# Bias addition and row maximum in one VectorE instruction, in the first block's attention

## The chip, the cores and the metric

The kernel runs on one core of one Trainium2 chip. The metric is device microseconds (us) of one execution. Engines are named as in the profile: PE is TensorE (PEld its weight load), DVE is VectorE, ACT is ScalarE, POOL is GpSimd and SP is SyncE, which issues most DMAs.

## The reference

A feed-forward layer, an attention layer, a second feed-forward layer and an embedding gate make up the first block; a second block of two layers follows. The change lies in the attention of the first block: 256 tokens, 16 heads of width 64. Heads 0 to 7 (mixer A) look at the last 128 tokens, share two key heads, and have a learned sink logit each; heads 8 to 15 (mixer B) merge three dilated windows.

```
logits = q @ k.T * 64 ** -0.5 + bias          # bias by distance, masked places at -1e30
m = max(logits)                               # mixer A: max(m, sink)
p = exp(logits - m)                           # mixer A: the denominator gets exp(sink - m) too
out = (p @ v) / sum(p)
att = concat(out of 16 heads) @ w_out + b_out
h = h + rms_norm(att, attn_post_g)
```

## The kernel before, in words

Everything is in f32. A projection is three matmuls per tile, on a high and a low part of each operand. `units` loads 128 x 2 x 512 of a weight by an SP DMA into one of four `raw` buffers, ACT rounds the high part (`whi`, L115) and DVE subtracts it (`wlo`, L116), into 16 `whl` buffers.

Attention of the first block (`attention1`) works in eight jobs of two heads: jobs 0 to 3 are mixer A (with the sink), jobs 4 to 7 mixer B. A job runs through these steps:

- `scores`: four matmuls into two PSUM tiles `S` (L443), one for each head, the first token tile in columns 0 to 127, the second in 128 to 383. DVE adds the bias and mask table `btab` (read backwards along the row) into `L` (L447, four instructions, two of 128 and two of 256 columns), takes row maxima (L449, one per token tile for both heads), takes the larger of that and the sink (L453, two instructions, mixer A alone), and negates (`nm`, L454). ACT takes exps with the row sums into `den` (L460, four). For mixer A the sink's exp joins `den` (L464 to L466). DVE takes the reciprocal `rc` (L468) and normalizes `L` (L473, four).
- `turn_p`, some time after: TensorE transposes `L` (L185) into a PSUM tile `trP`, three blocks a head, and ACT copies it to `pT` (L483).
- `apply`, after that: TensorE multiplies by the values into PSUM `O` (L491, L492); ACT and DVE split `O` into `mixh` (L190) and `mixl` (L191).

Behind jobs 0 to 3 two more projections each are put in (`fill`: q and k of mixer B, `z`). After the jobs come the matmuls with `w_out` (`wo`, L126 to L128): the first half of their inputs (jobs 0 to 3) for three of the four output tiles, then the second half, which needs jobs 4 to 7. Each output tile is finished by a bias addition on DVE (`att`, L571), and each token tile then goes through a norm into the next layer.

The PSUM tiles `S`, `O`, `z` and `wo` share six buffers (`mm`), `trP` has two (`tr`). When a step is issued, is set in the program by a clock that counts matmul rows (`spend`, `defer`, `WAIT`); the framework's scheduler then fixes one order of instructions for each engine when the program is built, by its own estimate of when each can start. The engines run these orders as they stand.

Of the kernel before, what the change touches and what calls it, by code (L numbers as in the profile page):

```python
# [14 lines left out]
ALU = mybir.AluOpType  # L15
AX = mybir.AxisListType.X
# [10 lines left out]
NEG = -1e30  # L27
# [15 lines left out]
class Net:  # L43
# [360 lines left out]
    def attention1(self, hs, norm, nxt):  # L404
        nc, a = self.nc, self.a
        X = norm.X
        snk = self.work.tile([P, 8], F32, name="snk", tag="snk", bufs=1)
# [24 lines left out]
        def scores(j, qT, kT, kj, sink):  # L432


            b0 = 2 * j if sink else 8 + 2 * j
            L = self.k4("L", [P, 2, 384])
            m = self.sm("m", 4)
            ps = [self.mm("S") for _ in range(2)]
            cs = [slice(0, 128), slice(128, 384)]
            for t in range(2):  # L440
                for i in range(2):
                    r = slice(64 * i, 64 * i + 64)
                    nc.tensor.matmul(ps[i][:, cs[t]], qT[r, j, t * P:(t + 1) * P], kT[r, kj, 0:128 * (t + 1)], start=True, stop=True)  # L443
            for t in range(2):
                for i in range(2):
                    b = b0 + i
                    nc.vector.tensor_tensor(out=L[:, i, cs[t]], in0=ps[i][:, cs[t]],  # L447
                                            in1=self.btab[b // 4][:, b % 4, 0:128 * (1 + t)][:, ::-1], op=ALU.add)
                nc.vector.tensor_reduce(out=m[:, 2 * t:2 * t + 2], in_=L[:, :, cs[t]], axis=AX, op=ALU.max)  # L449
            nm = self.sm("nm", 4)  # L450
            if sink:
                for t in range(2):
                    nc.vector.tensor_tensor(out=m[:, 2 * t:2 * t + 2], in0=m[:, 2 * t:2 * t + 2], in1=snk[:, 2 * j:2 * j + 2], op=ALU.max)  # L453
            nc.vector.tensor_scalar(out=nm, in0=m, scalar1=-1.0, scalar2=None, op0=ALU.mult)  # L454
            den = self.sm("den", 4)
            for t in range(2):
                o = slice(0, 128) if t == 0 else slice(128, 384)
                for i in range(2):
                    c = 2 * t + i
                    nc.scalar.activation(L[:, i, o], L[:, i, o], AF.Exp, bias=nm[:, c:c + 1], accum_out=den[:, c:c + 1])  # L460
            if sink:
                es = self.sm("es", 4)
                for t in range(2):
                    nc.vector.tensor_tensor(out=es[:, 2 * t:2 * t + 2], in0=nm[:, 2 * t:2 * t + 2], in1=snk[:, 2 * j:2 * j + 2], op=ALU.add)  # L464
                nc.scalar.activation(es, es, AF.Exp)
                nc.vector.tensor_tensor(out=den, in0=den, in1=es, op=ALU.add)  # L466
            rc = self.sm("rc", 4)
            nc.vector.reciprocal(rc, den)  # L468
            for t in range(2):
                o = slice(0, 128) if t == 0 else slice(128, 384)  # L470
                for i in range(2):
                    c = 2 * t + i
                    nc.vector.tensor_scalar(out=L[:, i, o], in0=L[:, i, o], scalar1=rc[:, c:c + 1], scalar2=None, op0=ALU.mult)  # L473
            return L
# [57 lines left out]
        def job(sa, ap):  # L532
            L = scores(*sa)
            self.spend(1900)

            def turn():
                pT = turn_p(L)
                self.clock += 0.7
                self.defer(lambda: apply(pT, *ap), WAIT["pv1"])

            self.defer(turn, WAIT["soft1"])
# [21 lines left out]
        for t in range(2):  # L563
            for n in range(2):
                ps = early.get((t, n))
                if ps is None:
                    ps = self.mm("wo")
# [957 lines left out]
```

## Time and profile before

| | us |
|---|---|
| three runs | 1761.73, 1761.76, 1766.66 (median 1761.76) |
| the profiled execution, its own time | 1764.69 |
| its span in the trace | 1761.7 |
| TensorE busy | 1721.5 |
| VectorE busy | 1248.3 |
| ScalarE busy | 864.4 |

The span is what the rows cover; the 3.0 us between it and the profiled execution's own time lie outside the trace. The attention stage of the first block lies between about 238 and 305 us of the span. A time in a row is counted from the span's start. A line number (L447) is that of the kernel's text; the kernel after has two lines fewer in `scores`, so that its L452 is L454 of before, L458 is L460, L471 is L473, L481 is L483 and L569 is L571.

### The profile page before, as it was taken

How to read it: one execution, taken by the hardware profiler on the slowest of the kernel's cores; microseconds unless marked ns; L12 is line 12 of the kernel's file. 1: busy time of each engine (PE TensorE's matmuls, PEld its weight loads, DVE VectorE, ACT ScalarE, POOL GpSimd, SP SyncE). 2: the span in 40 equal slices, each digit the busy share in tenths (PEclk: the TensorE clock that was granted, in tenths of full speed). 3: DMA queues.
4: the chain of work that ended last, by engine and by line, in shares of the span. 5: the costliest groups of instructions: out<-in, count | busy, mean ns of one | idle time of the engine just before them, and what ended most of it. 6: DMA issues, size and time to landing. Idle time of an engine off the chain costs nothing.

```text
span 1761.7 us, 26817 instructions
## 1 busy us (share of the span) xinstructions
PE 1721.5 (98%) x9910; PEld 1503.5 (85%) x9910; DVE 1248.3 (71%) x2467; ACT 864.4 (49%) x1809; POOL 49.4 (3%) x77
## 2 busy tenths in 40 slices
PE   7999999999999999999999999999999999999998
PEld 5998897889888888888878888887889988979997
DVE  6766778976769897687657886456659858775554
ACT  6444557654567442456425333333337446664443
POOL 0000000000001000110000000000000001000000
PEclk9999999999999999999999999999999999999999
DMA  7756644675564437422545566564334553465563
GB/s 271 256 196 205 216 153 144 217 251 197 171 205 149 145 134 261 152 85 84 191 168 179 190 224 232 174 217 155 116 124 143 167 191 124 147 225 195 186 202 111
DMA packets 96435, 315.14 MB, mean 179 GB/s; under 512 B 11006, under 2 KB 18608, under 8 KB 96304
## 3 DMA queue, kind: packets, MB, share of 16 engines
q1 hardware_dynamic: 94448, 309.73, 51.8%
q10 hardware_dynamic: 1856, 3.70, 0.6%
q8 instruction: 77, 1.26, 0.3%
q14 instruction: 54, 0.44, 0.1%
HBM read 300.76 MB, written 12.63 MB: 178 GB/s over the span
## 4 chain that ended last, share of the span: by engine, by line
PE 84%; DVE 6%; DMA 5%; ACT 2%; issue 2%; POOL 1%; SPq 0%; POOLq 0%; ACTq 0%; DVEq 0%
PE f2u L139 3%; PE f2u L141 3%; PE f2u L140 3%; PE f2dn L126 3%; PE f2g L139 3%; PE f2g L141 3%; PE f2g L140 3%; PE f2dn L128 3%; PE f2dn L127 3%; DVE wlo L116 2%; PE O L1145 2%; PE trP L185 1%; PE q L128 1%; PE q L126 1%; PE hy L139 1%
## 5 line engine op out<-in xcount | busy, mean ns | idle before, releaser
L116 DVE TENSOR_TENSOR wlo<-raw,whi 128x512 fp32r<-128x512 f32 x844 | 545.7, 683 | 149.0 <-ACT whi L115 106.4
L115 ACT ACTIVATE whi<-raw 128x512 fp32r<-128x512 f32 x844 | 492.8, 624 | 168.2 <-PE f2dn L128 29.6
L661 DVE SCALAR_TENSOR_TENSOR wmod<-wmod,crow 128x1024 f32<-128x1024 f32 x96 | 116.1, 1219 | 2.0 <-DMA wmod<-in_w_modT_dram 1.8
L126 PE MATMUL f2dn<-whi,f2ah 128*128 128x512 f32 x264 | 103.6, 392 | 0.0
L139 PE MATMUL f2g<-fxh,whi 128*128 128x512 f32 (+1 forms) x304 | 103.1, 339 | 0.0
L140 PE MATMUL f2g<-fxl,whi 128*128 128x512 f32 (+1 forms) x304 | 103.0, 339 | 0.0
L141 PE MATMUL f2g<-fxh,wlo 128*128 128x512 f32 (+1 forms) x304 | 103.0, 339 | 0.0
L139 PE MATMUL f2u<-fxh,whi 128*128 128x512 f32 (+1 forms) x304 | 103.0, 339 | 0.0
L140 PE MATMUL f2u<-fxl,whi 128*128 128x512 f32 (+1 forms) x304 | 103.0, 339 | 0.0
L141 PE MATMUL f2u<-fxh,wlo 128*128 128x512 f32 (+1 forms) x304 | 103.0, 339 | 0.0
L128 PE MATMUL f2dn<-whi,f2al 128*128 128x512 f32 x264 | 102.8, 389 | 0.0
L127 PE MATMUL f2dn<-wlo,f2ah 128*128 128x512 f32 x264 | 102.7, 389 | 0.0
L661 DVE SCALAR_TENSOR_TENSOR mjunk<-wmod,crow 128x1024 bf16<-128x1024 f32 x64 | 77.4, 1219 | 10.9 <-DMA wmod<-in_w_modT_dram 10.7
L141 PE MATMUL hy<-lxh,wlo 128*128 128x256 f32 (+1 forms) x224 | 69.7, 315 | 0.1
L140 PE MATMUL hy<-lxl,whi 128*128 128x256 f32 (+1 forms) x224 | 69.6, 314 | 0.0
L139 PE MATMUL hy<-lxh,whi 128*128 128x256 f32 (+1 forms) x224 | 69.2, 316 | 0.0
L190 ACT ACTIVATE f2ah<-f2s 128x512 fp32r<-128x512 f32 (+1 forms) x40 | 21.3, 532 | 91.3 <-DVE f2s L288 91.2
L285 ACT ACTIVATE f2s<-f2g 128x512 f32<-128x512 f32 (+1 forms) x38 | 18.9, 496 | 95.2 <-PE f2g L141 95.2
L288 DVE TENSOR_TENSOR f2s<-f2u,f2s 128x512 f32<-128x512 f32 (+1 forms) x38 | 21.4, 562 | 60.7 <-PE f2u L141 60.7
L140 PEld LDWEIGHTS f2g<-fxl,whi 128*128 128x128 f32 x304 | 57.7, 190 | 6.3
L141 PEld LDWEIGHTS f2u<-fxh,wlo 128*128 128x128 f32 x304 | 57.7, 190 | 6.3
L139 PEld LDWEIGHTS f2u<-fxh,whi 128*128 128x128 f32 x304 | 57.7, 190 | 6.2
(527 smaller groups left out, 4785.4 us busy)
## 6 DMA issues: line engine op xcount, KB each, us to landing
wmod<-in_w_modT_dram SPq DMA_DIRECT2D x96, 512.0 KB, 6.4
raw<-in_ffn_w_gu_dram SPq DMA_DIRECT2D x88, 512.0 KB, 4.6
raw<-in_w_gate_up_dram SPq DMA_DIRECT2D x88, 512.0 KB, 5.9
raw<-in_w_in_dram SPq DMA_DIRECT2D x80, 512.0 KB, 5.1
raw<-in_ffn_w_down_dram SPq DMA_DIRECT2D x44, 512.0 KB, 4.6
raw<-in_w_down_dram SPq DMA_DIRECT2D x44, 512.0 KB, 4.0
raw<-in_w_out_dram SPq DMA_DIRECT2D x24, 512.0 KB, 4.7
raw<-in_w_in_q_dram SPq DMA_DIRECT2D x16, 512.0 KB, 5.1
```

Source lines behind the costliest of these rows:

```text
L115: nc.scalar.activation(hi, raw[:, j], AF.Copy)
L116: nc.vector.tensor_tensor(out=lo, in0=raw[:, j], in1=hi.bitcast(F32), op=ALU.subtract)
L126: nc.tensor.matmul(ps[:, :n], xh, hi, start=first and k == 0, stop=False)
L127: nc.tensor.matmul(ps[:, :n], xh, lo, start=False, stop=False)
L128: nc.tensor.matmul(ps[:, :n], xl, hi, start=False, stop=last and k == z)
L139: nc.tensor.matmul(ps[:, m], hi[:, c], xh, start=first and k == 0, stop=False)
L140: nc.tensor.matmul(ps[:, m], hi[:, c], xl, start=False, stop=False)
L141: nc.tensor.matmul(ps[:, m], lo[:, c], xh, start=False, stop=last and k == z)
L190: nc.scalar.activation(hi, ps, AF.Copy)
L288: nc.vector.tensor_tensor(out=s, in0=pu[:, :W], in1=s, op=ALU.mult)
L661: nc.vector.scalar_tensor_tensor(out=junk, in0=w, scalar=1.0, in1=self.crows[s], op0=ALU.mult, op1=ALU.mult, accum_out=self.modc[layer][s] ...
L1145: nc.tensor.matmul(po[:, :256], V[:, kt, g * P:(g + 1) * P], pT[:, k, :], start=k == 0, stop=k == nt - 1)
```

## The change

The four bias additions, the two row maxima and, in mixer A, the two maxima with the sink of a job become four `tensor_tensor_reduce` instructions, one for each head and token tile. Each adds the table to the scores, writes `L`, and folds the row maximum into one column of `m`, starting from the sink's column (mixer A) or from -1e30 (mixer B).

```diff
--- before.py
+++ after.py
@@ -444,13 +444,11 @@
             for t in range(2):
                 for i in range(2):
                     b = b0 + i
-                    nc.vector.tensor_tensor(out=L[:, i, cs[t]], in0=ps[i][:, cs[t]],
-                                            in1=self.btab[b // 4][:, b % 4, 0:128 * (1 + t)][:, ::-1], op=ALU.add)
-                nc.vector.tensor_reduce(out=m[:, 2 * t:2 * t + 2], in_=L[:, :, cs[t]], axis=AX, op=ALU.max)
+                    nc.vector.tensor_tensor_reduce(out=L[:, i, cs[t]], in0=ps[i][:, cs[t]],
+                                                   in1=self.btab[b // 4][:, b % 4, 0:128 * (1 + t)][:, ::-1], scale=1.0,
+                                                   scalar=snk[:, 2 * j + i:2 * j + i + 1] if sink else NEG, op0=ALU.add, op1=ALU.max,
+                                                   accum_out=m[:, 2 * t + i:2 * t + i + 1])
             nm = self.sm("nm", 4)
-            if sink:
-                for t in range(2):
-                    nc.vector.tensor_tensor(out=m[:, 2 * t:2 * t + 2], in0=m[:, 2 * t:2 * t + 2], in1=snk[:, 2 * j:2 * j + 2], op=ALU.max)
             nc.vector.tensor_scalar(out=nm, in0=m, scalar1=-1.0, scalar2=None, op0=ALU.mult)
             den = self.sm("den", 4)
             for t in range(2):
```

In the built program each of these stands as two DVE instructions, both named ISA: the main one, and a 128x1 one that writes the column of `m`. DVE has 56 instructions fewer of the old kinds in the eight jobs (32 additions, 16 row maxima, 8 maxima with the sink) and 64 of the new ones. The order of SP and of POOL is the same as before; outside the attention stage so is the order of all engines. Inside it the scheduler chose another order on DVE, ACT and TensorE.

On VectorE, from the bias additions of job 4 on, this stood before. `L_3260`, `L_3287` and `L_3325` belong to jobs 4, 5 and 6, and so do `S`, `m` and `nm` next to them; a row with x2 stands for two instructions alike.

```order
L447 TENSOR_TENSOR L_3260<-S_3262,btab_1973 128x128
L447 TENSOR_TENSOR L_3260<-S_3262,btab_1973 128x256
L447 TENSOR_TENSOR L_3260<-S_3263,btab_1973 128x128
L447 TENSOR_TENSOR L_3260<-S_3263,btab_1973 128x256
L449 TENSOR_REDUCE m_3261<-L_3260 128x2 x2
L447 TENSOR_TENSOR L_3287<-S_3289,btab_1973 128x128
L454 TENSOR_SCALAR nm_3274<-m_3261 128x4
L447 TENSOR_TENSOR L_3287<-S_3290,btab_1973 128x128
L447 TENSOR_TENSOR L_3287<-S_3289,btab_1973 128x256
L447 TENSOR_TENSOR L_3287<-S_3290,btab_1973 128x256
L447 TENSOR_TENSOR L_3325<-S_3327,btab_1975 128x128
```

In the kernel after, job 4 is `L_3244` and job 5 `L_3269`; its rows from `nm` of job 4 on are these.

```order
L452 TENSOR_SCALAR nm_3256<-m_3245 128x4
L116 TENSOR_TENSOR wlo_3401<-raw_3398,whi_3400 128x512
L116 TENSOR_TENSOR wlo_3405<-raw_3398,whi_3404 128x512
L116 TENSOR_TENSOR wlo_3411<-raw_3408,whi_3410 128x512
L116 TENSOR_TENSOR wlo_3415<-raw_3408,whi_3414 128x512
L466 RECIPROCAL rc_3263<-den_3258 128x4
L447 ISA L_3269,m_3270<-S_3271,btab_1973 128x128
L447 ISA m_3270 128x1
L471 TENSOR_SCALAR L_3244<-L_3244,rc_3263 128x128 x2
L471 TENSOR_SCALAR L_3244<-L_3244,rc_3263 128x256 x2
L447 ISA L_3269,m_3270<-S_3272,btab_1973 128x128
L447 ISA m_3270 128x1
```

The additions of jobs 5 and 6 stood right behind those of job 4; now job 5's first one stands behind job 4's reciprocal, and the other three behind job 4's normalization. Jobs 6 and 7 follow in the same pattern, each behind the job before it.

On ScalarE the copies of job 4's transposed tile (`pT_3495`) stood here before; job 5 is `L_3287`, job 6 `L_3325`.

```order
L460 ACTIVATE L_3287,den_3303<-L_3287,nm_3301 128x128 x2
L460 ACTIVATE L_3287,den_3303<-L_3287,nm_3301 128x256 x2
L98 DMA row_attn_post_g_3388<-in_attn_post_g_dram 128x1024
L483 ACTIVATE pT_3495<-trP_3496 128x384
L483 ACTIVATE pT_3495<-trP_3501 128x384
L483 ACTIVATE pT_3509<-trP_3510 128x384
L460 ACTIVATE L_3325,den_3341<-L_3325,nm_3339 128x128 x2
```

In the kernel after, job 4's copies are `pT_3471`; jobs 5, 6 and 7 are `L_3269`, `L_3305` and `L_3330`.

```order
L458 ACTIVATE L_3269,den_3283<-L_3269,nm_3281 128x256 x2
L190 ACTIVATE mixh_2406<-O_3355 128x256
L115 ACTIVATE whi_3444<-raw_3438 128x512
L458 ACTIVATE L_3305,den_3319<-L_3305,nm_3317 128x128 x2
L458 ACTIVATE L_3305,den_3319<-L_3305,nm_3317 128x256 x2
L98 DMA row_b_out_3362<-in_b_out_dram 128x1024
L98 DMA row_attn_post_g_3364<-in_attn_post_g_dram 128x1024
L458 ACTIVATE L_3330,den_3344<-L_3330,nm_3342 128x128 x2
L458 ACTIVATE L_3330,den_3344<-L_3330,nm_3342 128x256 x2
L481 ACTIVATE pT_3471<-trP_3472 128x384
L481 ACTIVATE pT_3471<-trP_3477 128x384
```

Job 4's copies stood behind the exps of job 5; now they stand behind those of job 7.

On TensorE the transposes of job 5 (`trP_3510`) stood among the `wo` matmuls before, and job 4's O (`O_3520`) right behind them.

```order
L185 MATMUL trP_3496<-ident_75,L_3260 128x128 x3
L128 MATMUL wo_3472<-whi_3408,mixl_2408 128x512
L185 MATMUL trP_3501<-ident_75,L_3260 128x128 x3
L127 MATMUL wo_3485<-wlo_3435,mixh_2406 128x512
L128 MATMUL wo_3485<-whi_3434,mixl_2408 128x512
L126 MATMUL wo_3485<-whi_3438,mixh_2406 128x512
L185 MATMUL trP_3510<-ident_75,L_3287 128x128 x3
L491 MATMUL O_3520<-pT_3495,vB_2523 64x256
L127 MATMUL wo_3485<-wlo_3439,mixh_2406 128x512
```

In the kernel after, the transposes of job 4 stand ahead of job 3's O, 24 `wo` matmuls follow, and these are the last of them and what comes next (`trP_3486` is job 5's, `O_3496` job 4's).

```order
L126 MATMUL wo_3461<-whi_3424,mixh_2406 128x512
L127 MATMUL wo_3461<-wlo_3425,mixh_2406 128x512
L128 MATMUL wo_3461<-whi_3424,mixl_2408 128x512
L185 MATMUL trP_3486<-ident_75,L_3269 128x128 x3
L185 MATMUL trP_3491<-ident_75,L_3269 128x128 x3
L489 MATMUL O_3496<-pT_3471,vB_2523 64x256
L490 MATMUL O_3496<-pT_3471,vB_2606 64x128
```

Job 5's transposes moved from the middle of the `wo` matmuls to behind 24 of them, and everything of the second half of `w_out` stands behind them.

## Rows read from the trace of the kernel before

**Rows 1.** The page: busy us (share of span) and instructions by engine.

```profile
PE 1721.5 (98%) x9910; PEld 1503.5 (85%) x9910; DVE 1248.3 (71%) x2467; ACT 864.4 (49%) x1809; POOL 49.4 (3%) x77
```

**Rows 2.** Stretches: us, busy (count) by engine, PEclk, DMA share, GB/s.

```profile
240.00:273.00 33.00, 32.95 (x269) 29.45 (x270) 25.83 (x91) 18.80 (x59) 0.00 (x0) 1.00 0.32 106
273.00:292.00 19.00, 17.21 (x105) 12.00 (x105) 18.77 (x57) 12.74 (x40) 0.00 (x0) 0.91 0.57 194
...
310.00:340.00 30.00, 28.80 (x142) 23.15 (x142) 27.28 (x58) 20.00 (x48) 1.74 (x3) 1.00 0.63 218
284.00:285.00 1.00, 1.00 (x4) 0.70 (x3) 1.00 (x5) 0.00 (x0) 0.00 (x0) 0.50 0.63 213
```

**Rows 3.** VectorE by shape, 238 to 305 us: busy us, mean ns, idle us.

```profile
L447 DVE TENSOR_TENSOR L<-S,btab 128x256 f32<-128x256 f32 x16 | 6.4, 414 | 0.0
...
L447 DVE TENSOR_TENSOR L<-S,btab 128x128 f32<-128x128 f32 x16 | 4.3, 284 | 1.1 <-PE S L443 1.1
...
L453 DVE TENSOR_TENSOR m<-m,snk 128x2 f32<-128x2 f32 x8 | 1.2, 154 | 0.0
```

**Rows 4.** VectorE's timeline at 718 us: start us, us, what, idle before it.

```profile
718.63 1.22 DVE L661 SCALAR_TENSOR_TENSOR mjunk<-wmod,crow 128x1024 bf16<-128x1024 f32 x1
719.78 0.08 DVE L661 DVE_READ_ACCUMULATOR mjunk<-wmod,crow 128x1 f32 x1
719.78 0.69 DVE L116 TENSOR_TENSOR wlo<-raw,whi 128x512 fp32r<-128x512 f32 x1
```

**Rows 5.** VectorE's timeline, jobs four and five, and the first half's bias.

```profile
273.78 1.15 DVE L447 TENSOR_TENSOR L<-S,btab 128x128 f32<-128x128 f32 x4
274.85 1.00 DVE L449 TENSOR_REDUCE m<-L 128x2 f32<-128x256 f32 x2
275.76 0.28 DVE L447 TENSOR_TENSOR L<-S,btab 128x128 f32<-128x128 f32 x1
...
278.22 0.18 DVE L468 RECIPROCAL rc<-den 128x4 f32<-128x4 f32 x1 [0.19 <-ACT L L460]
...
278.62 1.00 DVE L473 TENSOR_SCALAR L<-L,rc 128x128 f32<-128x128 f32 x4
279.54 0.68 DVE L449 TENSOR_REDUCE m<-L 128x2 f32<-128x512 f32 x1
...
281.60 1.89 DVE L116 TENSOR_TENSOR wlo<-raw,whi 128x512 fp32r<-128x512 f32 x3
283.40 0.17 DVE L468 RECIPROCAL rc<-den 128x4 f32<-128x4 f32 x1
...
303.75 0.69 DVE L571 TENSOR_TENSOR att<-wo,row_b_out 128x512 f32<-128x512 f32 x1 [0.85 <-PE wo L128]
```

**Rows 6.** ScalarE's timeline, exps and copies of jobs four and five.

```profile
276.34 0.40 ACT L460 ACTIVATE L<-L,nm 128x128 f32<-128x128 f32 x1
...
282.30 0.84 ACT L483 ACTIVATE pT<-trP 128x384 f32<-128x384 f32 x2
```

**Rows 7.** The chain of waits, 269 to 276 us: start us, us, what.

```profile
270.19 4.27 DMA raw<-in_w_out_dram
```

**Rows 8.** TensorE's timeline in the same stage.

```profile
281.73 0.50 PE L128 MATMUL wo<-whi,mixl 128*128 128x512 f32 x1 [0.74 <-DVE mixl L191]
...
283.54 0.65 PE L127 MATMUL wo<-wlo,mixh 128*128 128x512 f32 x1 [0.98 <-DVE wlo L116]
...
296.26 0.87 PE L185 MATMUL trP<-ident,L 128*128 128x128 f32 x6
297.06 0.32 PE L492 MATMUL O<-pT,vB 128*64 128x128 f32 x1
...
297.87 0.50 PE L127 MATMUL wo<-wlo,mixh 128*128 128x512 f32 x1
...
303.09 0.39 PE L127 MATMUL wo<-wlo,mixh 128*128 128x512 f32 x1
303.32 0.39 PE L128 MATMUL wo<-whi,mixl 128*128 128x512 f32 x1
```

## The prediction

> **What bounds the kernel now.** I read the page first, for the engine that is busy longest: TensorE, 98% of the span [rows 1]. A change on VectorE (71%) can therefore move the time only where TensorE stands still or runs slowly. So the second view was the busy times by stretch over the attention stage [rows 2]. From 240 to 273 us, where jobs 0 to 3 lie beside the projections of q and k, TensorE is busy 32.95 of 33.00 us: VectorE is covered there, whatever it costs. From 273 to 292 us it is the other way round: VectorE is busy 18.77 of 19.00 us, TensorE 17.21, and its granted clock is 0.91 on average. [...] From 310 us on TensorE is busy 28.80 of 30.00 again, so I take a delay that reaches there as carried to the end.
>
> The third view was the timelines of that stretch. TensorE waits 0.74 us for a mixl and 0.98 us for a wlo, both VectorE's [rows 8]; VectorE at that time is working through additions, maxima and normalizations of jobs 4 to 7 one after the other [rows 5]. The stage's end for what follows is the bias addition of the first token tile's second half, at 303.75 us, which waited for TensorE [rows 5].
>
> **What the change takes from VectorE.** A job's four additions take 273.78 to 274.85 = 1.07 us, the two row maxima 274.85 to 275.76 = 0.91 [rows 5], the two maxima with the sink 2 x 0.154 = 0.31 [rows 3]. So a job of mixer A costs 2.29 us, one of mixer B 1.98.
>
> No row shows the new instruction. Its main part reads and writes what the addition did, so I put it at the addition's 1.07 us for four; below that I see no reason, since every element is still read and written once. The 128x1 part behind it has one relative in the trace: an instruction of L661 that also accumulates is followed by an accumulator read of 0.08 us, and the next instruction starts in the same hundredth as this read [rows 4]. A read thus costs 0 to 0.08 us; I take 0.05. Four pairs: 1.07 + 0.20 = 1.27 us (1.07 to 1.39). Upwards the bound is an instruction that needs two passes: an element costs (414 - 284) / 128 = 1.02 ns in an addition [rows 3], a job has 768 elements, hence 0.78 us more. I stay by the accumulating row of L661: 1.22 us for 1024 elements of f32 [rows 4] is one pass.
>
> [...]
>
> The saving is 1.02 us a job in mixer A, all under a busy TensorE and worth nothing, and 0.71 in mixer B: 4 x 0.71 = 2.8 us of VectorE's work in the stretch that it bounds. Were the order unchanged, this would be a gain.
>
> **What the change moves.** The order is not unchanged, and this decides my forecast. Before, the additions of jobs 5 and 6 stood right behind job 4's, so the scores of one job were ready while another's exps ran. After, jobs 5, 6 and 7 each have their first addition behind the reciprocal of the job before, and the others behind its normalization: a chain. In it ScalarE's exps cost 276.34 to 278.22 = 1.88 us from their start to the reciprocal [rows 5, 6], and from the reciprocal to the next job's nm VectorE has 0.10 (reciprocal) + 0.25 (first pair) + 278.62 to 279.54 = 0.92 (normalization [rows 5]) + 1.0 (three pairs) = 2.27 us, and what weight work stands between. I walk it, with 0.60 us a wlo (281.60 to 283.40 is three [rows 5]):
>
> - Job 4: one wlo now stands ahead of it, 273.78 + 0.60 = 274.4 start; 1.27 + a wlo 0.60: nm at 276.25. Four wlo follow, so the reciprocal is at about 276.35 + 4 x 0.60 = 278.75, later than its exps (278.4).
> - Job 5: 278.75 + 2.27 + 0.60 (a wlo) = 281.6 for nm. But ahead of its exps ScalarE has a whi whose raw buffer comes free with the second of those four wlo, at 277.55; a load in this place takes 4.27 us [rows 7], the rounding 0.5: 282.3. The reciprocal comes at 282.3 + 1.88 = 284.2.
> - Job 6: 284.2 + 2.27 + 0.3 (a mixl, half a wlo's columns) = 286.8; exps from 287.0, reciprocal 288.9.
> - Job 7: 288.9 + 2.27 = 291.15; exps from 291.35 to 293.1.
>
> **Who waits for it.** Job 4's pT copies now stand behind the exps of job 7 on ScalarE, where before they started at 282.30 [rows 6]. So they start at 293.1; the first is done after 0.84 / 2 = 0.42 us, and frees one of the two trP buffers for job 5's transposes, at about 293.55. Everything else of the second half of w_out is queued behind those on TensorE. Ahead of them it has the 24 wo. The last 13 need a PSUM tile that job 6's additions release, at about 286.1, and at 303.32 - 303.09 = 0.23 us each [rows 8] they are through at 289.1. From there TensorE has nothing for 4.4 us. It has another gap of some 2.7 us at 277 to 279.7, as job 4's transposes, now ahead of job 3's O, wait for the normalization.
>
> From 293.55: transposes and O of jobs 5 to 7 go through two trP buffers. A job has 0.80 us of transposes by six (296.26 to 297.06) and 0.81 of O (297.06 to 297.87) [rows 8], and I add 0.3 for the copy that neither covers: 1.9 a job, three times, and 0.42 + 0.8 = 1.2 for the last copy and the last O: 293.55 + 5.7 + 1.2 = 300.45. By the order 30 wo then remain to the bias addition: 30 x 0.23 = 6.9, so 307.35, against 303.75: **+3.6 us**.
>
> To this comes the clock. [...] After 0.98 us idle the clock fell in the kernel before [rows 2, 8]; the new gap is longer and I expect the same behind it, but there TensorE waits for copies half the time anyway. I take **+1.0** (0 to 1.8). Jobs 0 to 3, SP and POOL: 0, under TensorE's 32.95 of 33.00. If TensorE weren't full there, the 4 x 1.02 us would be a gain.
>
> The sum is +4.6 us: the profiled execution's span would go from 1761.7 to 1766.3, its own time from 1764.69 to 1769.3. That execution is 2.9 us above the median of the runs shown, so for the median I add the same 4.6 to 1761.76: **1766.4 us**. Uncertain are the round of 1.9 (1.6 to 2.2, so 0.9 either way), the start of the chain (1 us either way) and the clock; together 1764 to 1769.
>
> **The rivals.**
>
> The gain comes through. VectorE is the bound from 273 to 292 us, it gets 2.8 us less to do, and TensorE's 1.79 us idle and 1.7 us at half clock are what can be had: at most 3.5, I take 3.0, 1758.8 us. For it: TensorE's two waits there end with VectorE. Against it: job 4's copies stand behind job 7's exps. The point from which it decides is the start of job 5's transposes: each microsecond before 293.55 takes one off, and at 293.55 - 3.6 = 289.95 nothing is lost; the chain would have to be 3.6 us shorter over four jobs.
>
> Both cancel, 1761.8 us: the chain's latency and the saved work come out even, for instance if the exps of job 5 start at 281.0 instead of 282.3 and a job's round is 1.3. [...]
>
> The new instruction is slow: two passes and full reads, 0.78 + 0.27 = 1.05 us more a job, four jobs on the chain: +4.2 on top of 4.6, 1770.6 us. For it: no row shows it, and it is built as an instruction of its own kind. Against: the row of L661.
>
> **How the numbers follow.** The forecast (slower by 3 to 7 us) gets 0.55, the gain 0.12, no change 0.15, the slow instruction 0.18. A measurement of this kernel can tell about 0.3% from no change, which is 5.3 us: below 1756.5 is faster, above 1767.0 slower. Of the forecast 0.33 lies below 1767.0 and 0.22 above; the slow instruction is all above: 0.40. The gain lies at the edge, 0.04 beyond 1756.5 if it also takes what I hold for covered, the rest of it, 0.08, within; with no change's 0.15 the middle has 0.56. The range reaches from the gain's 1759 to 1772, past the slow instruction's 1770.6; the forecast's own is 1764 to 1769.
>
> **What would show it.** In the profile after: four pairs of job 4 taking 1.27 us start to start; reads next to free; job 5's additions behind job 4's reciprocal, and exps of jobs 4 to 7 some 4.5 us apart; a gap of TensorE of about 4 us that ends with a pT copy near 293.5; the first half's last bias addition (L569) at about 307 to 308; and the rest of the rows shifted by as much. Wrong it would be if that gap were under 1 us, if the addition with the maximum took clearly more than the plain one, or if the later stages took the delay back.

## The result, and the profile after

| | before | after |
|---|---|---|
| median of six runs | 1761.82 | 1771.49 us |
| span of the profiled execution | 1761.7 | 1768.8 us |
| TensorE busy between 273 and 292 us | 17.21 | 11.86 us |

The change makes the kernel slower: ratio 1.0052, with a 95% interval of 1.0041 to 1.0063, or 9.2 us (7.2 to 11.1). The stretches of the kernel after, in the columns of [rows 2]:

```profile
240.00:273.00 33.00, 33.00 (x268) 29.34 (x268) 22.05 (x89) 18.73 (x59) 0.00 (x0) 1.00 0.28 93
273.00:292.00 19.00, 11.86 (x77) 8.25 (x76) 16.04 (x65) 11.35 (x38) 0.00 (x0) 1.00 0.71 223
292.00:310.00 18.00, 16.08 (x81) 11.13 (x82) 6.66 (x15) 9.64 (x25) 0.00 (x0) 0.81 0.24 84
310.00:340.00 30.00, 28.75 (x134) 22.62 (x133) 25.71 (x56) 21.96 (x54) 2.89 (x4) 1.00 0.39 126
```

The kernel before, from 292 to 310 us:

```profile
292.00:310.00 18.00, 18.00 (x87) 13.40 (x85) 12.00 (x24) 12.76 (x34) 1.15 (x2) 1.00 0.29 98
```

Jobs 0 to 3 cost TensorE nothing in their own stretch in either kernel: it is full from 240 to 273 us, and VectorE's busy time fell from 25.83 to 22.05 us under it. From 273 to 292 us TensorE is busy 5.35 us less, and from 292 to 310 another 1.92 us less, with a granted clock of 0.81 where the kernel before has 18.00 us and 1.00. The new instruction is not the reason. VectorE's rows of it by shape (busy us, mean ns, idle before), against [rows 3]:

```profile
L447 DVE CUSTOM_DVE_ANT_0 L<-S,btab,snk 128x256 f32<-128x256 f32 x8 | 3.7, 480 | 0.0
...
L447 DVE CUSTOM_DVE_ANT_0 L<-S,btab 128x256 f32<-128x256 f32 x8 | 3.1, 418 | 0.0
L447 DVE DVE_READ_ACCUMULATOR2_ANT m<- 128x1 f32 x32 | 2.6, 82 | 0.0
L447 DVE CUSTOM_DVE_ANT_0 L<-S,btab,snk 128x128 f32<-128x128 f32 x8 | 2.6, 349 | 0.7 <-PE S L443 0.7
L447 DVE CUSTOM_DVE_ANT_0 L<-S,btab 128x128 f32<-128x128 f32 x8 | 2.1, 274 | 0.0
```

The plain addition took 414 and 284 ns, the new one takes 418 and 274 without the sink. With the sink's column as its start it is dearer, 480 and 349. The read is 82 ns long, but the next instruction starts with it, as in the timeline of jobs 4 and 5:

```profile
274.06 0.28 DVE L447 CUSTOM_DVE_ANT_0 L<-S,btab 128x128 f32<-128x128 f32 x1
274.27 0.08 DVE L447 DVE_READ_ACCUMULATOR2_ANT m<- 128x1 f32 x1
274.27 0.28 DVE L447 CUSTOM_DVE_ANT_0 L<-S,btab 128x128 f32<-128x128 f32 x1
...
275.17 0.69 DVE L116 TENSOR_TENSOR wlo<-raw,whi 128x512 fp32r<-128x512 f32 x1
...
278.25 0.17 DVE L466 RECIPROCAL rc<-den 128x4 f32<-128x4 f32 x1
278.34 0.26 DVE L447 CUSTOM_DVE_ANT_0 L<-S,btab 128x128 f32<-128x128 f32 x1
...
278.52 1.00 DVE L471 TENSOR_SCALAR L<-L,rc 128x128 f32<-128x128 f32 x4
279.44 0.28 DVE L447 CUSTOM_DVE_ANT_0 L<-S,btab 128x128 f32<-128x128 f32 x1
...
280.94 0.16 DVE L452 TENSOR_SCALAR nm<-m 128x4 f32<-128x4 f32 x1
...
284.63 0.18 DVE L466 RECIPROCAL rc<-den 128x4 f32<-128x4 f32 x1 [1.06 <-ACT L L458]
...
289.16 0.18 DVE L466 RECIPROCAL rc<-den 128x4 f32<-128x4 f32 x1 [1.34 <-ACT L L458]
...
291.37 0.17 DVE L452 TENSOR_SCALAR nm<-m 128x4 f32<-128x4 f32 x1
293.53 0.18 DVE L466 RECIPROCAL rc<-den 128x4 f32<-128x4 f32 x1 [1.99 <-ACT L L458]
```

Four pairs of job 4 take 274.06 to 275.17 = 1.11 us, where additions and maxima took 1.98 [rows 5]. But behind job 4's reciprocal (278.25) there is one addition of job 5, then the normalization, then the other three: its nm comes at 280.94. The reciprocals of jobs 4 to 7 are 6.4, 4.5 and 4.4 us apart. ScalarE, in the same stretch:

```profile
282.21 0.63 ACT L115 ACTIVATE whi<-raw 128x512 fp32r<-128x512 f32 x1 [1.14 <-DMA raw<-in_w_out_dram]
...
291.63 0.40 ACT L458 ACTIVATE L<-L,nm 128x128 f32<-128x128 f32 x1 [2.51 <-DVE nm L452]
...
293.40 0.84 ACT L481 ACTIVATE pT<-trP 128x384 f32<-128x384 f32 x2
```

A whi that waits 1.14 us for its load holds job 5's exps until 282.75; job 7's begin at 291.63, and only behind them, at 293.40, come job 4's copies, which began at 282.30 before [rows 6]. TensorE:

```profile
279.70 0.93 PE L185 MATMUL trP<-ident,L 128*128 128x128 f32 x6 [2.85 <-ACT pT L481]
...
293.92 1.54 PE L185 MATMUL trP<-ident,L 128*128 128x128 f32 x6 [4.16 <-ACT pT L481]
295.39 1.13 PE L489 MATMUL O<-pT,vB 128*64 128x256 f32 x4
...
300.97 0.50 PE L126 MATMUL wo<-whi,mixh 128*128 128x512 f32 x1
...
301.86 0.66 PE L489 MATMUL O<-pT,vB 128*64 128x256 f32 x4
...
304.37 0.50 PE L126 MATMUL wo<-whi,mixh 128*128 128x512 f32 x1
```

It waits 2.85 us ahead of job 4's transposes and 4.16 us ahead of job 5's, then runs six transposes in 1.47 us (293.92 to 295.39) where they took 0.80 [rows 8]: the granted clock is 0.50, its lower level, from 293 to 299 us. The first token tile's second bias addition:

```profile
311.50 0.69 DVE L569 TENSOR_TENSOR att<-wo,row_b_out 128x512 f32<-128x512 f32 x1 [1.30 <-PE wo L128]
```

It comes at 311.50, against 303.75 [rows 5]: 7.75 us, of which 7.1 us are left at the end of the spans.

### The profile page after: what moved, and what is told of

Same layout as the page of the kernel before. It is cut to its first block, busy times and chain, and to the rows that moved or that the text cites. A ratio compares the mean times of both kernels' runs of the same rounds, so it can differ in the third digit from the quotient of the medians.

```text
span 1768.8 us, 26826 instructions
## 1 busy us (share of the span) xinstructions
PE 1721.9 (97%) x9910; PEld 1502.8 (85%) x9910; DVE 1242.1 (70%) x2475; ACT 865.1 (49%) x1809; POOL 49.4 (3%) x77
## 4 chain that ended last, share of the span: by engine, by line
PE 85%; DMA 5%; DVE 5%; ACT 2%; issue 1%; POOL 1%; SPq 0%; POOLq 0%; ACTq 0%; DVEq 0%
PE f2u L141 3%; PE f2u L140 3%; PE f2u L139 3%; PE f2dn L126 3%; PE f2g L141 3%; PE f2g L140 3%; PE f2g L139 3%; PE f2dn L128 3%; PE f2dn L127 3%; PE O L1143 2%; DVE wlo L116 2%; PE hy L141 1%; PE hy L139 1%; PE hy L140 1%; DMA raw<-in_w_gate_up_dram 1%
## 5 line engine op out<-in xcount | busy, mean ns | idle before, releaser
L139 PEld LDWEIGHTS f2g<-fxh,whi 128*128 128x128 f32 x304 | 57.7, 190 | 6.3
```

Of the source, the lines that this page charges most:

```text
L139: nc.tensor.matmul(ps[:, m], hi[:, c], xh, start=first and k == 0, stop=False)
```

## The experiments

Theory 1: the loss is the order, since additions queued behind the reciprocal of the job before make a chain of jobs 4 to 7. Theory 2: the loss is the instruction. For each run, with its ratio to before, the table gives the length of the stage in its one trace, from the start of the last kTB on VectorE (the keys of mixer B, the last projection ahead of job 4) to that second bias addition, and TensorE's mean granted clock from 273 to 310 us:

| run | stage us | clock | median us | ratio (95%) |
|---|---|---|---|---|
| before | 30.46 | 0.95 | 1761.82 | |
| E8, before again | 29.70 | 1.00 | 1763.18 (one execution) | |
| after | 38.44 | 0.91 | 1771.49 | 1.0052 (1.0041 to 1.0063) |
| E1, new for mixer A | 33.57 | 0.95 | 1767.00 | 1.0030 (1.0019 to 1.0040) |
| E2, new for mixer B | 36.87 | 0.86 | 1771.32 | 1.0055 (1.0040 to 1.0070) |
| E3, old in the chain | 42.34 | 0.82 | 1773.04 | 1.0066 (1.0050 to 1.0082) |
| E4, own buffers for m | 32.29 | 1.00 | 1769.81 | 1.0050 (1.0033 to 1.0066) |
| E11, the same again | 35.03 | 0.91 | 1771.94 (one execution) | |
| E5, new in the old order | 27.86 | 1.00 | 1761.34 | 0.9999 (0.9989 to 1.0009) |
| E6, old in the new order | 41.77 | 0.82 | 1778.96 | 1.0093 (1.0075 to 1.0111) |
| E7, zeros in the gap | 36.00 | 0.95 | 1770.14 | 1.0048 (1.0033 to 1.0062) |
| E9, E4 and early copies | 29.39 | 0.95 | 1762.82 | 1.0004 (0.9995 to 1.0014) |
| E10, old and early copies | 31.60 | 0.95 | 1761.41 | 0.9999 (0.9990 to 1.0007) |

**E1 and E2: one mixer each.** `if sink:` (E1) or `if not sink:` (E2) around the new instructions, the old ones in the other branch.

> The new instruction in jobs 0 to 3 alone; jobs 4 to 7 keep the addition and the maximum. Theory 1 (the loss is the order of jobs 4 to 7, additions queued behind the reciprocal of the job before): no loss, 1760 to 1764 us, ratio to before 0.999 to 1.001. Theory 2 (the instruction itself is dearer wherever it stands, 32 of them cost 9.7 us): half of the loss, about 1766.6 us, ratio 1.003.

> The new instruction in jobs 4 to 7 alone. Theory 1: the whole loss, 1769 to 1773 us, ratio 1.004 to 1.006, with a gap of TensorE of about 4 us that ends near 293 us with job 4's copies. Theory 2: half, about 1766.6 us, ratio 1.003.

E2 has the whole loss, as theory 1 has it, with a gap of 4.91 us ended by job 4's copies at 293.79. E1 missed theory 1's number and met that of theory 2. Its trace gives a reason other than the instruction. Jobs 4 to 7 have the old instructions, and on VectorE jobs 5 and 6 have their additions ahead of job 4's reciprocal as before, but ScalarE's order moved with jobs 0 to 3; its timeline:

```profile
275.37 0.87 ACT L494 ACTIVATE pT<-trP 128x384 f32<-128x384 f32 x2 [0.97 <-PE trP L185]
278.15 0.63 ACT L115 ACTIVATE whi<-raw 128x512 fp32r<-128x512 f32 x1 [1.90 <-DMA raw<-in_w_out_dram]
...
278.69 0.39 ACT L471 ACTIVATE L<-L,nm 128x128 f32<-128x128 f32 x1
```

A whi now stands between job 3's copies and job 4's exps and waits 1.90 us for its load, so that the exps start at 278.69 instead of 276.34 [rows 6]; TensorE then waits 1.57 and 1.76 us at 283.9 and 286.4. That this is all of E1's loss isn't shown. E1's 5.7 us and E2's 10.1 make more than the 9.7 of both together, so the two mixers' losses don't add up as terms of a sum.

**E3: the old instructions in the chain.** An edge of order, without a wait for data:

```
add = nc.vector.tensor_tensor(out=L[:, i, cs[t]], ..., op=ALU.add)
if self.rc1 is not None:
    self.tc.add_manual_dep(add.ins, self.rc1.ins.name, <NoSync>)
...
self.rc1 = nc.vector.reciprocal(rc, den)
```

> The old instructions, with an edge of order (no wait for data) that puts each job's additions behind the reciprocal of the job before on VectorE, as the new kernel's stand. Theory 1: a loss without the new instruction, 1766 to 1773 us, ratio 1.003 to 1.006; the gap of TensorE behind 24 wo may be shorter than in the new kernel, since half of job 4's copies stand ahead of job 7's exps. Theory 2: 1761.8 us, ratio 1.000 (0.999 to 1.001).

1773.04 us, just above the range: the chain costs 11.8 us without the new instruction. The reciprocals of jobs 4 to 7 come at 280.85, 287.85, 293.17 and 298.54, the last two of these rows:

```profile
293.17 0.18 DVE L471 RECIPROCAL rc<-den 128x4 f32<-128x4 f32 x1 [1.93 <-ACT L L463]
...
298.54 0.18 DVE L471 RECIPROCAL rc<-den 128x4 f32<-128x4 f32 x1 [1.99 <-ACT L L463]
```

TensorE waits 3.83, 1.56 and 4.03 us for copies, and its clock is 0.82 and 0.81 in both stretches, where the kernel after has 1.00 and 0.81; the 11.8 us are the price of this chain, not that of the kernel after.

**E4 and E11: buffers of its own for m.** In the kernel before, m, nm, den, es and rc share one ring of buffers, which the framework hands out in the order of the program: the row maxima of job 5, the first to write m, stood behind job 4's reciprocal there too, and the additions did not. Now the addition writes m.

```
-            m = self.sm("m", 4)
+            m = self.small.tile([P, 4], F32, name="m", tag="m4", bufs=8)
```

> The new instruction in all jobs, but the tile m of the maxima has buffers of its own instead of sharing a ring with den and rc, so that it gets its buffer without waiting in line behind the rc of the job before. Theory 1: the additions of job n+1 are queued ahead of job n's reciprocal, the chain is gone, and job 4's copies, still behind job 7's exps, start near 288 instead of 293.4 us: 1764 to 1768 us, ratio to before 1.001 to 1.003. Theory 2: 1771 us, ratio 1.005.

> The kernel of e4 once more, for a second trace: its five timed executions took 1768 to 1774 us, the profiled one 1762.3, of which the attention stage shows 4 us more than in the kernel before. If the stage itself is what varies: this execution, if it is over 1766 us, has the first token tile's last bias addition later than 307.5 us, by a longer gap or by TensorE's lower clock between 284 and 300 us. If what varies lies outside: the addition is within 1 us of the 306.6 us of e4's trace, and the granted clock or idle time differ behind 340 us.

In the built program this line alone puts all four additions of job 5 ahead of job 4's reciprocal; that is where the order came from. On the chip it helped little: 1769.81 us, nearly 2 us above the range. The reciprocals are early (job 7's at 287.76 instead of 293.53), but the new order has another fault, on ScalarE:

```profile
285.86 0.40 ACT L458 ACTIVATE L<-L,nm 128x128 f32<-128x128 f32 x1 [1.30 <-DVE nm L452]
...
287.63 2.70 ACT L115 ACTIVATE whi<-raw 128x512 fp32r<-128x512 f32 x5
290.23 0.84 ACT L481 ACTIVATE pT<-trP 128x384 f32<-128x384 f32 x2
```

Five whi of 2.6 us now stand ahead of job 4's copies, which start at 290.23. And E4's trace is of its fastest execution (1762.31, the others 1768 to 1774), with the clock whole; E11's, 1771.94 us, lies beside it (E4's two stretches first, then E11's):

```profile
273.00:292.00 19.00, 14.93 (x94) 10.45 (x93) 18.17 (x72) 15.12 (x49) 0.00 (x0) 1.00 0.58 186
292.00:310.00 18.00, 18.00 (x97) 13.25 (x97) 8.37 (x15) 9.68 (x21) 0.55 (x1) 1.00 0.40 127
```

```profile
273.00:292.00 19.00, 15.35 (x98) 11.26 (x96) 18.18 (x75) 15.30 (x50) 0.00 (x0) 0.97 0.57 179
292.00:310.00 18.00, 17.75 (x86) 11.84 (x85) 6.96 (x13) 8.36 (x18) 0.00 (x0) 0.84 0.45 144
```

The same order and nearly the same waits of TensorE (E4: 1.08, 0.70, 1.06, 0.84 us; E11: 1.08, 0.70, 1.04, 0.84), but in E11 a granted clock of 0.50 from 291 to 297 us, where E4 has 1.00: the stage is 2.7 us longer. E11 also reached the stage 1.3 us later, and another 5 us between these two executions lie behind 340 us, in stretches that both have. E4's stage is 2.6 us longer than E8's, E11's 5.3; the 8.5 us that E4 loses in the median are not explained by the stage alone.

**E5 and E6: each instruction in the other's order.** A table of numbers lists, for VectorE, ScalarE and TensorE, the other kernel's order in the attention stage, and an edge of order ties each instruction to the one in front. E5 has E4's line too.

> The new instruction in all jobs, and VectorE, ScalarE and TensorE pinned by edges of order to the order that the kernel before has in the attention stage (m with buffers of its own, without which that order can't be had). Theory 1 (order): the loss is gone and some of VectorE's 2.8 us in jobs 4 to 7 comes through: 1758 to 1761.5 us, ratio 0.998 to 1.000. Theory 2 (the instruction): 1767 to 1771 us, ratio over 1.003. A third, that the saved work is hidden anyway: 1761.3 us, ratio 1.000.

> The mirror of it: the old additions, row maxima and sink maxima, pinned to the order of the changed kernel, each maximum right behind its additions. Theory 1: the new kernel's loss of 10 us, and 0.71 us more for each of jobs 5, 6 and 7 on the chain: about 1773.5 us (1771 to 1776), ratio 1.0055 to 1.008. Theory 2: 1761.3 us, ratio 1.000.

These decide it. The new instruction in the old order: no loss, 0.9999. The old instructions in the new order: 1.0093. E6's reciprocals, of jobs 4 to 7, on VectorE:

```profile
281.90 0.17 DVE L488 RECIPROCAL rc<-den 128x4 f32<-128x4 f32 x1
...
288.19 0.17 DVE L488 RECIPROCAL rc<-den 128x4 f32<-128x4 f32 x1
...
293.84 0.18 DVE L488 RECIPROCAL rc<-den 128x4 f32<-128x4 f32 x1 [1.35 <-ACT L L480]
...
299.34 0.18 DVE L488 RECIPROCAL rc<-den 128x4 f32<-128x4 f32 x1 [1.99 <-ACT L L480]
```

They are 6.3, 5.7 and 5.5 us apart. TensorE's gap then ends at 299.73:

```profile
299.73 1.54 PE L205 MATMUL trP<-ident,L 128*128 128x128 f32 x6 [5.49 <-ACT pT L503]
```

E6 loses more than was expected (17.4 us, not 10 and 2). Part of it lies in jobs 0 to 3: from their first addition to the last kTB it takes 33.07 us (242.52 to 275.59), the kernel after 30.58, so that these 2.5 us don't belong to the chain of jobs 4 to 7. Its clock was 0.82 and 0.81 in two stretches, not one, and by how much that adds was not taken apart. In E5 TensorE has one wait left in the stage:

```profile
284.52 0.50 PE L146 MATMUL wo<-wlo,mixh 128*128 128x512 f32 x1 [0.98 <-DVE wlo L135]
```

and, by stretch:

```profile
273.00:292.00 19.00, 18.02 (x124) 13.45 (x123) 17.69 (x73) 15.13 (x49) 0.00 (x0) 1.00 0.62 200
292.00:310.00 18.00, 17.54 (x85) 12.99 (x83) 12.06 (x25) 12.89 (x35) 1.48 (x2) 1.00 0.35 114
```

VectorE is busy 17.69 us of 19.00 where it was 18.77. The stage is 1.8 us shorter than in E8 and 2.6 shorter than in the first trace, but the time is not: 0.2 us less, with an interval of 1.9 less to 1.6 more. E5's traced execution reached the stage 2.4 us later than E8's; job 0's first addition was already 3.0 us later (245.54 against 242.52), from stretches that the change doesn't touch. Whether a gain of 1 to 2 us is there stays open.

**E7: the clock.** 18 matmuls on a zero tile behind the 24 wo:

```
+            if (t, n) == (0, 1):
+                for _ in range(18):
+                    nc.tensor.matmul(early[t, n], self.zero, us[n][0][0], start=False, stop=False)
```

> The changed kernel with 18 more matmuls on a zero tile behind the 24 wo, 18 x 0.2275 = 4.1 us, which fill TensorE's gap before job 5's transposes and add zero to the result. If 5.4 us at the lower clock behind that gap cost 2.7 us: the granted clock stays at its upper level from 292 to 300 us, the bias addition of the first token tile's second half comes at 309 instead of 311.5 us, and the time is 1768 to 1770 us, ratio to before 1.004. If the clock doesn't matter there: 1771.5 us, ratio 1.0055 or a little more.

```profile
288.62 4.28 PE L564 MATMUL wo<-whi,zero 128*128 128x512 f32 x18
292.93 0.55 PE L187 MATMUL trP<-ident,L 128*128 128x128 f32 x3
...
301.65 0.50 PE L128 MATMUL wo<-whi,mixh 128*128 128x512 f32 x1
```

```profile
292.00:310.00 18.00, 17.97 (x97) 12.51 (x97) 8.04 (x17) 9.28 (x22) 0.00 (x0) 1.00 0.22 69
```

With TensorE kept busy to 292.93 the clock is at its upper level, 1.00, from 292 to 310 us, and from the first transpose of job 5 to the end of job 7's O it needs 301.65 - 292.93 = 8.72 us, where the kernel after needs 304.37 - 293.92 = 10.45: the lower clock costs 1.73 us there, not 2.7. This is as near as two traces tell it, since E7's first O matmuls stand between job 5's transposes and not behind them. The bias addition came at 308.78, as expected. The median of 1770.14, just above the range, is 1.4 us lower than after's, which the intervals can't tell from none.

**E8: before again.**

> The kernel before, unchanged, for a second trace of it. If its profiled execution (1764.69 us, 3.4 above the median of its runs) lost time outside the attention stage: the stage's rows agree within 0.3 us (bias additions at 301.5 and 303.75), and granted clock or idle time differ in later stretches, above all 920 to 940 and 1360 to 1400 us. Otherwise the stage itself differs.

```profile
273.00:292.00 19.00, 16.71 (x107) 11.71 (x104) 18.78 (x58) 13.00 (x42) 0.00 (x0) 1.00 0.57 193
```

```profile
302.70 0.69 DVE L571 TENSOR_TENSOR att<-wo,row_b_out 128x512 f32<-128x512 f32 x1 [0.85 <-PE wo L128]
```

The addition came 1.05 us earlier: 0.29 us of this were there at the last kTB, and 0.76 arose in the stage, which has no drop of the clock here (1.00 from 273 to 292 us, against 0.91 in [rows 2]; the first trace has 0.50 from 284 to 287). Behind 340 us the two executions differ both ways: the first is 3.3 us later at 935 us, 2.1 at 1569 and 0.3 at the end. E8's execution is itself above the median, so where the rest of the 3.4 us lay isn't shown. Against this trace the kernel after is 311.50 - 302.70 = 8.8 us late; that distance stays between 7.7 and 9.1 through to 1575 us, and the spans end 7.4 us apart.

**E9 and E10: a better order.** `with self.tc.high_priority(200):` around `turn_p`, on E4 and on the kernel before.

> The new instruction, m with buffers of its own, and a higher priority for the transposes and copies of each job, which puts job 4's copies ahead of job 7's exps again. If these two places of order were all of the loss: job 4's copies start near 283 us, TensorE has no gap over 1.5 us between 273 and 292, and the time is 1758 to 1761.5 us, ratio to before 0.998 to 1.000. If the loss has a third place: over 1763 us.

> The old instructions with the same higher priority, the fair counterpart: a gain of e9 over before that this kernel has too would be the priority's, not the instruction's. Expected 1760 to 1763 us, ratio 0.999 to 1.001, 1 to 3 us above e9 if the 2.8 us that VectorE saves in jobs 4 to 7 come through.

Both come out as before. E9 takes back nearly all of the loss with two changes of the text, at 1762.82 us above its range: job 4's copies start at 282.92, as expected, but TensorE still waits 1.88 us for a normalization at 279.4. That VectorE's saving comes through there is not seen, since E10 isn't slower. No version beat the kernel before by more than the noise.

## Why the prediction was right or wrong

Right in its direction and its mechanism; too small by half: 4.6 us against 9.2. The measured 1771.49 us lies above the forecast's own 1764 to 1769. The wider range reached to 1772 only for the rival of the slow instruction, which the runs refute, so that the time still falls inside it is luck. By its steps:

- **The instruction.** Four pairs at 1.27 us: 1.11 without the sink (the reads hide wholly: the next instruction starts with each, at 274.27, 274.48, 274.83 and 275.17), 242.48 to 243.83 = 1.35 with it. That is no second pass, for which I had put 0.78 us more a job: the slow-instruction rival, which had met the measured time best (1770.6), is out, by the rows above and by E5. The cost of a sink's column, 62 to 75 ns an instruction, I had not seen coming.
- **Mixer A, worth nothing.** Its own work yes (32.95 and 33.00 us of 33.00); but E1 loses 5.7 us with the change in mixer A alone, and there ScalarE's order behind it moved. I had put nothing there.
- **The chain.** Reciprocals forecast at 278.75, 284.2 and 288.9: 278.25, 284.63 and 289.16. Job 4's copies at 293.1: 293.40. Job 5's transposes at 293.55: 293.92. The gap of 4.4 us: 4.16. E3 and E6 show that the chain costs time without the new instruction, E5 that the instruction costs none without the chain. Where the order came from I had not said; E4's line shows the ring of buffers.
- **From job 5's transposes to the end of job 7's O**, 5.7 + 1.2 = 6.9 us: this term was too small. At full clock it takes 8.72 (E7). Missing are two groups of three wo that stand ahead of job 6's and job 7's O (300.97 to 301.86 and the like: 0.89 each, 1.78 together). That the remaining 6.94 us meet my 6.9 is luck in part: in E7 the rounds of jobs 5 and 6 take 2.34 and 1.38 us (transposes at 292.93, 295.27 and 296.65), where I had 1.9 for each.
- **The clock**, +1.0 (0 to 1.8): at 0.50 from 293 to 299 us it cost 1.73 (against E7), near the upper bound.
- **The end**: 307.35 forecast, 311.50 measured. The later start gives 0.37, the step above 8.72 - 6.9 = 1.82, the clock 1.73, and the 30 wo take 7.13 instead of 6.9, 0.23 more: together the 4.15 us. Of the 1.73, the forecast had 1.0 in a term of its own.
- **The base.** The first trace of before has a drop of the clock in this very stage, which another execution doesn't have (E8). I read it as 1.7 us lost (19.00 x 0.09, from the mean of 0.91 [rows 2]), part of what the gain rival could win back; without it the stage is 0.76 us shorter. A sum against the first trace alone comes out too small: 7.75 us instead of 8.8 against E8, and 9.2 is measured.
- **The gain rival** gave 3.0 us. E5 has its condition fulfilled (the old order and the saved work) and its interval allows at most 1.9 us. "Both cancel" is out too: the loss is 7.2 us at least.

## What to carry to other kernels

A fused instruction that writes its second result earlier also claims that result's buffer earlier, and where buffers are handed out in program order, this can queue it behind work of the step before (E4: with buffers of its own for m, job 5's additions stand ahead of job 4's reciprocal again); look at the order that the build chose before counting what an instruction saves. To tell an instruction's cost from the order's, build each in the other's order (E5, E6). Where a wait of TensorE grows by microseconds, price a lower clock behind it too (in the kernel after 0.50 from 293 to 299 us behind the wait of 4.16 us, worth 1.73 us; 1.00 behind that of 2.85 us), and count every instruction that stands between, not only those of the chain.

## What the runs showed of the hardware

Two executions of one program can differ in a stage by the clock alone: E4 and E11 have the same waits of about a microsecond each, and from 291 to 297 us one runs at a granted clock of 1.00, the other at 0.50; the stage is 2.7 us longer. Executions of one kernel lie up to 11 us apart (E4: 1762.31 to 1773.61); how much of that is the clock in all stretches together was not summed. A trace of one execution can show a stage at either level.
